# The x of the SSD head groups turned to tokens by VectorE block transposes and DRAM instead of TensorE, and the C·B products moved into a later visit

## The chip, the cores and the metric

The kernel runs on one core of a Trainium2 chip. The time is that of the device in microseconds, for one execution of the whole program. The core has TensorE (PE, matmul), VectorE (DVE), ScalarE (ACT), GpSimd (POOL) and SyncE (SP); each has its own queue of instructions, which it takes in order, and semaphores join them. ACT, POOL and SP also issue DMA transfers.

## The reference, cut to what matters

One inference step of one decoder layer. 256 prompt tokens and 8 samples of 8 new tokens (320 tokens in all) with a width of 2048 go through one input projection, then through two kinds of head groups (a gated chunk MLP and a state space mixer), an output projection and a convolutional FFN.

```python
def decoder_layer(x, ...):
    h = rms_norm(x, norm_mix_pre)
    proj = h @ w_in                              # [a_u | a_v | z | x,B,C | dt]
    gate_out = chunk_spatial_gate(a_u, a_v, ...)
    ssm_out = ssd_mixer(z, xbc, dt_raw, ...)
    x = x + rms_norm(concat([gate_out, ssm_out]) @ w_out, norm_mix_post)
    return x + rms_norm(conv_ffn(rms_norm(x, ...), ...), ...)

def ssd_mixer(...):
    xbc = silu(causal_depthwise_conv(xbc))       # x: 2048 = 32 heads x 64, B and C: 4 groups x 128
    dt, a = softplus(dt_raw + dt_bias), -exp(a_log)
    ...                                          # y = ssd_scan(...) + d * x, times silu(z), RMS norm per group

def ssd_scan(x, dt, a, bm, cm, init_state):      # per chunk of 128 tokens
    xdt = x * dt                                 # token by token, head by head
    cb = einsum(C_t, B_s)                        # per group, tokens x tokens
    y_diag = (cb * decay) @ xdt
    states = einsum(B, decay_states, xdt)        # summed over the tokens of a chunk
    y_off  = C @ states_in * exp(da_cs)
```

The 32 heads form four groups of eight heads; a group shares its B and C. All sums here run over tokens, so x is wanted with tokens on the partitions, while the projection leaves it with features on the partitions and tokens along the row.

## The kernel before

**The stream of weights.** All matrix products with weights are done in three float32r products: each operand is split into a rounded part and a rest, and whi·xhi, whi·xlo and wlo·xhi are added up in PSUM (`accumulate`, lines 134 to 136). Weights come in slabs of 512 KB (`slab`): SP loads one (`wraw`), ACT rounds it (`whi`, line 123), VectorE subtracts (`wlo`, line 124). There are three buffers of each, and a slab feeds 24 matmuls of 128 x 320. `project` computes columns of the input projection or of the FFN's up projection into four PSUM banks, with an eviction function for each (`scaled`, whose evictions `ev` are line 393). `chunk_out` takes four blocks of 128 rows of the output or the down projection; its 16 column blocks (`pd`) are added by VectorE to an accumulator in SBUF (line 247).

**Side work.** Everything else is written as generators that stand in two lists. Behind each slab, `tick` lets the tasks of `side` and the first one of `bg` go one step further. A task yields a pair: how many matmuls of weights have to be made before its next step, and how many have to be left in the running projection. `finish` drives a task to its end. `tc.issue_after` keeps an instruction behind a given one.

**Order of the stages around the change.** First come the v columns, dt, B and C, then the gate stage: x of group 0 is projected (`heads_in(0)`, which leaves it in a tile `xs`, features on partitions), and four gate groups follow, each with a projection of u (`gate_up`), the mixing inside chunks (`gate_mix`, which loads `wT` by POOL at line 786 and multiplies it by a mask at line 791) and a `chunk_out`. Then the four SSD groups: while the generator `ssd(g)` runs as a background task, the stream computes x of group g+1 (`heads_in_next`), `chunk_out` of an earlier group and z of group g (`heads_out`).

**B.** B is turned to tokens before the gate stage by `to_tokens`: for each of five blocks of 64 tokens VectorE transposes 32 x 32 squares (line 421) into a tile of the tag `pv` (four buffers, which evictions use too), and POOL writes it in four DMAs of 32 KB to DRAM (`b_d`, line 423), from where POOL loads rows of tokens (`b_raw`, line 831). B of the samples, four times repeated (`b4`, lines 839 to 843), is loaded in the gate stage.

**One SSD group, `ssd(g)`.** It works in visits between slabs.

- Visit one: for each of the two prompt chunks TensorE transposes four blocks of `xs` into PSUM (`by_token`, line 415), VectorE multiplies by dt out of PSUM (`times`, line 911, into `xdt`), and POOL makes a decayed copy of the first (`x0d`, line 916). Then the four products of C and B (lines 946 and 949), and their masks on VectorE. Before it, ACT writes the samples' x four times side by side (`fourfold`, line 432).
- Visit two, 48 matmuls later or more: eight transposes of that fourfold copy into two PSUM banks, the state's product of the first chunk (`s1`, line 968, from `x0d`), and 32 small products of C with the samples' states (line 977). Its PSUM is multiplied by dt for the samples (`samples_split`, `samples_rows`).
- Then 13 short steps n = 0 to 12 (12 for group 3): decays, the samples' new states (`grown`), and at n = 6 and n = 12 the products of y (line 1058). After them POOL makes `x1d`, the decayed copy of the second chunk (`decayed(1, 1)`), and SP stores it with `s1` for groups 0 to 2 (`x1_d`, `s1_d`); `load_ends` brings them back before the last chunk of the output projection.

Group 0 has a further visit in between, for `b_of_samples` (lines 860 to 867).

## Time and profile before

| | us |
|---|---|
| three runs | 1757.96, 1758.81, 1760.32 |
| median | 1758.81 |
| the profiled execution | 1759.16 |
| its span in the trace | 1757.5 |
| VectorE busy | 1171.2 |
| ScalarE busy | 826.8 |
| GpSimd busy | 325.5 |

The span goes from the first to the last instruction of the profiled execution; 1.66 us of its time lie around it. "Busy" is the sum of an engine's instructions; PE stands for TensorE's matmuls, PEld for its weight loads, which overlap them. The list of waits gives for each engine and line what ended its idle time. A group of instructions is given as line, engine, operation, output and inputs, the count, the busy time and the mean duration of one in nanoseconds, then the idle time ahead of it. In the timeline a row begins with the start and the time taken in microseconds; a count over one joins instructions in sequence, and a bracket gives the idle time before them and what ended it.

### The profile page before, as it was taken

Reading aid. Unit: us, or ns where it says so; the run is one execution under the profiler, and the core shown is the slowest. Engines: PE = TensorE matmul, PEld = TensorE weight load, DVE = VectorE, ACT = ScalarE, POOL = GpSimd, SP = SyncE. Lnnn points to the kernel's source line nnn. Section 1 sums busy time; section 2 is a strip of 40 time slices with the busy share of each in tenths; the row PEclk is TensorE's granted clock in tenths of the full one; section 3 lists DMA queues with packets and bytes.
Section 4 is the critical chain, followed back from the end, with each engine's and each line's share of the span. In section 5 each row is a group of like instructions: output and inputs, shape, how many; then the busy total and the mean of one; then the engine's idle time right before and its main releaser. Section 6 shows DMA issues by size and latency. Waiting matters only on the chain.

```text
span 1757.5 us, 31257 instructions
## 1 busy us (share of the span) xinstructions
PE 1748.8 (100%) x12129; PEld 1727.8 (98%) x12129; DVE 1171.2 (67%) x2004; ACT 826.8 (47%) x1218; POOL 325.5 (19%) x687
## 2 busy tenths in 40 slices
PE   9999999999999999999999999999999999999998
PEld 9999999999999999999999999999999999999998
DVE  6548863656969787778855566565657565656575
ACT  5444545334656565645544434343434343333445
POOL 2432330000413323111210101010201010101004
PEclk9999999999999999999999999999999999999999
DMA  7786554456676676665654545545554545454542
GB/s 236 228 239 186 181 175 148 153 164 191 194 217 204 213 220 188 213 196 161 187 157 146 157 147 156 148 151 153 154 149 149 155 149 155 149 155 147 155 150 106
DMA packets 229108, 302.26 MB, mean 172 GB/s; under 512 B 21344, under 2 KB 154336, under 8 KB 228768
## 3 DMA queue, kind: packets, MB, share of 16 engines
q1 hardware_dynamic: 213488, 274.09, 51.4%
q0 software_dynamic: 5888, 12.79, 2.5%
q10 hardware_dynamic: 9584, 13.38, 2.1%
q8 instruction: 96, 1.57, 0.4%
q14 instruction: 52, 0.43, 0.1%
HBM read 280.51 MB, written 19.69 MB: 171 GB/s over the span
## 4 chain that ended last, share of the span: by engine, by line
PE 60%; DVE 0%; issue 0%; ACT 0%; ACTq 0%
PE ps L134 13%; PE ps L136 12%; PE ps L135 12%; PE pd L135 7%; PE pd L136 7%; PE pd L134 7%; PE x1p L1402 0%; PE fin_ps L1130 0%; PE y_ps L1058 0%; PE tsum L292 0%; PE ps_other L136 0%; PE ps_other L134 0%; PE ps_other L135 0%; PE ps L188 0%; PE yo_ps L977 0%; PE up_ps L994 0%
## 5 line engine op out<-in xcount | busy, mean ns | idle before, releaser
L124 DVE TENSOR_TENSOR wlo<-wraw,whi 128x1024 fp32r<-128x1024 f32 (+2 forms) x480 | 582.9, 1215 | 418.2 <-ACT whi L123 414.0
L123 ACT CAST whi<-wraw 128x1024 fp32r<-128x1024 f32 (+2 forms) x479 | 495.6, 1035 | 663.9 <-PE ps L135 382.6
L134 PE MATMUL ps<-h_hi,whi 128*128 128x320 f32 x2428 | 750.8, 310 | 0.6 <-DVE acc_mix L247 0.6
L135 PE MATMUL ps<-h_lo,whi 128*128 128x320 f32 x2428 | 749.2, 309 | 0.0
L136 PE MATMUL ps<-h_hi,wlo 128*128 128x320 f32 x2428 | 748.5, 309 | 0.0
L134 PEld LDWEIGHTS ps<-h_hi,whi 128*128 128x128 f32 x2428 | 455.8, 188 | 3.5 <-issue 0.8
L135 PEld LDWEIGHTS ps<-h_lo,whi 128*128 128x128 f32 x2428 | 456.0, 188 | 0.4
L136 PEld LDWEIGHTS ps<-h_hi,wlo 128*128 128x128 f32 x2428 | 455.8, 188 | 0.0
L135 PE MATMUL pd<-flo,whi 128*128 128x320 f32 x704 | 217.2, 308 | 0.0
L136 PE MATMUL pd<-fhi,wlo 128*128 128x320 f32 x704 | 217.2, 308 | 0.0
L134 PE MATMUL pd<-fhi,whi 128*128 128x320 f32 x704 | 217.1, 308 | 0.0
L134 PE MATMUL pd<-ohi,whi 128*128 128x320 f32 x448 | 138.9, 310 | 0.1
L135 PE MATMUL pd<-olo,whi 128*128 128x320 f32 x448 | 138.4, 309 | 0.0
L136 PE MATMUL pd<-ohi,wlo 128*128 128x320 f32 x448 | 138.4, 309 | 0.0
L135 PEld LDWEIGHTS pd<-flo,whi 128*128 128x128 f32 x704 | 132.2, 188 | 0.0
L136 PEld LDWEIGHTS pd<-fhi,wlo 128*128 128x128 f32 x704 | 132.2, 188 | 0.0
L134 PEld LDWEIGHTS pd<-fhi,whi 128*128 128x128 f32 x704 | 132.2, 188 | 0.0
L1304 POOL COPY ptf<-pad 128x2 f32<-128x2 f32 x88 | 21.0, 238 | 599.6 <-DVE pad L1292 598.9
L247 DVE TENSOR_TENSOR acc_ffn<-acc_ffn,pd 128x320 f32<-128x320 f32 (+1 forms) x161 | 77.6, 482 | 37.2 <-PE pd L136 35.7
L134 PEld LDWEIGHTS pd<-ohi,whi 128*128 128x128 f32 x448 | 84.1, 188 | 0.9 <-PE pd L136 0.3
L135 PEld LDWEIGHTS pd<-olo,whi 128*128 128x128 f32 x448 | 84.1, 188 | 0.3
L136 PEld LDWEIGHTS pd<-ohi,wlo 128*128 128x128 f32 x448 | 84.1, 188 | 0.0
(339 smaller groups left out, 1756.1 us busy)
## 6 DMA issues: line engine op xcount, KB each, us to landing
wraw<-in_ffn_w_up SPq DMA_DIRECT2D x176, 512.0 KB, 3.6
wraw<-in_w_in SPq DMA_DIRECT2D x132, 512.0 KB, 3.9
wraw<-in_ffn_w_down SPq DMA_DIRECT2D x88, 512.0 KB, 3.3
wraw<-in_w_out SPq DMA_DIRECT2D x64, 512.0 KB, 3.4
st<-in_state_ssm SPq DMA_DIRECT2D x40, 256.0 KB, 4.3
out_ssm_state_sample<-st ACTq DMA_DIRECT2D x30, 256.0 KB, 2.5
cs<-dacs_d SPq DMA_DIRECT2D x16, 320.0 KB, 4.8
wraw<-in_w_in SPq DMA_DIRECT2D x12, 384.0 KB, 3.6
```

What stands on the lines that cost most here:

```text
L123: rounded[:] = [act.copy(hi, raw).ins]
L124: dve.tensor_tensor(out=lo, in0=raw, in1=hi.bitcast(F32), op=ALU.subtract)
L134: pe.matmul(ps, whi, xhi, start=first, stop=False)
L135: pe.matmul(ps, whi, xlo, start=False, stop=False)
L136: last_made[0] = pe.matmul(ps, wlo, xhi, start=False, stop=last).ins
L247: added_last[:] = [dve.tensor_tensor(out=acc[:, nb, ts], in0=acc[:, nb, ts], in1=ps[:, ts], op=ALU.add).ins]
L1304: pool.tensor_copy(ptf[:, k, :], pad[:, 256:258])
```

## The change

x of every group goes the way that B went: block transposes on VectorE, 20 POOL writes of 32 KB to DRAM (`x_d`, one tile for each group), and POOL loads of rows of tokens. `to_tokens` gets the writing function as an argument and runs as a task of `side`. The 64 transposes of TensorE and the eight fourfold copies of ACT are gone; `times` reads SBUF, in two halves, with the features in the order in which the block transposes leave them. Group 0's rows are loaded in the gate stage, where B of the samples was; that load moves into `ssd(0)` and `b_of_samples` behind visit two. For the other groups the rows are asked for at step n = 11 of the group before. The products of C and B move from visit one into visit two, their masks behind it; the multiplications of the samples move ahead of it. `x1d` is made and stored at n = 3.

```diff
+    x_d = [dr.tile([NT, 512], F32, name=f"x_d{g}") for g in range(4)]
...
-    def by_token(ps, x, c):
-
-        pe.transpose(ps, x[:, P * c:P * c + P], ident)
+    def by_pool(rows, o, t):
+
+        for i in range(4):
+            pool.dma_start(rows[o:o + NS, P * i:P * i + P].rearrange("(r t) f -> t r f", t=32), t[32 * i:32 * i + 32])
-    def to_tokens(x, rows):
+    def to_tokens(x, rows, by):
...
+            by(rows, o, t)
             yield
...
             finish(b_turned)
+            x_turned = {0: to_tokens(x0, x_d[0], by_pool)}
+            side.append(x_turned[0])
...
                     if g == 2:
-                        b4 = [[tp.tile([P, NT], F32, tag="pv", name="b4", bufs=4)[:, :256] for _ in range(2)] for _ in range(2)]
+                        finish(x_turned[0])
+                        x_raw = [[tp.tile([P, NT], F32, tag="pv", name="x_raw", bufs=4)[:, :256] for _ in range(2)] for _ in range(2)]
+                        for c in range(2):
                             for h in range(2):
-                                pool.dma_start(b4[i][h], b_d[o:o + 32, 256 * h:256 * h + 256].unsqueeze(0).broadcast_to([4, 32, 256]))
+                                pool.dma_start(x_raw[c][h], x_d[0][P * c:P * c + P, 256 * h:256 * h + 256])
...
+            def load_x_tokens(g):
+
+                raw = [sd.tile([P, 512], F32, tag="xde", name="x_raw", bufs=2) for _ in range(2)]
+                for c in range(2):
+                    pool.dma_start(raw[c], x_d[g][P * c:P * c + P])
+                return [[raw[c][:, 256 * h:256 * h + 256] for h in range(2)] for c in range(2)]
+
+            def load_x_samples(g):
+
+                x4 = sd.tile([P, 2, 512], F32, tag="xsp", name="x4", bufs=1)
+                for i in range(2):
+                    o = NP + 32 * i
+                    pool.dma_start(x4[:, i], x_d[g][o:o + 32].unsqueeze(0).broadcast_to([4, 32, 512]))
+                return x4
+
+            tokens_of = {0: x_raw}
+            samples_of = {0: load_x_samples(0)}
...
-                def times(out, ps, c, at=slice(0, P), h=slice(0, 8)):
+                def times(out, raw, c, h, at=slice(0, P), js=slice(0, 4)):
+
+                    n = js.stop - js.start
+                    o = out.rearrange("p (j h i f) -> p h j i f", j=4, h=2, f=32)[:, h, js]
+                    d = dt[at, c, h0:h0 + 8].rearrange("p (j h) -> p h j", h=2)[:, h, js]
+                    dve.tensor_tensor(out=o, in0=raw.rearrange("p (i j f) -> p j i f", j=4, f=32)[:, js],
+                                      in1=d.unsqueeze(2).unsqueeze(3).to_broadcast([at.stop - at.start, n, 2, 32]), op=ALU.mult)
...
+                raw = tokens_of.pop(g)
                 for c in range(2):
-                    ps = misc("xt_ps")
-                    for j in range(4):
-                        by_token(ps[:, P * j:P * j + P], xs[:, j], c)
-                    times(xdt[:, c, :], ps, c)
+                    for h in range(2):
+                        times(xdt[:, c, :], raw[c][h], c, h)
                     if c == 0:
                         x0d = decayed(0, 0)
-                ps = misc("cb_ps")
-                ...
...
+                yield 24, 0
                 if g == 0:
+                    b4 = load_b()
                     yield 48, 0
-                    with tc.issue_after(last_made[0]):
-                        b_of_samples()
-                yield 48, 72
-
-                ps_x = [x_of_samples(i) for i in range(2)]
+                with tc.issue_after(last_made[0]):
+                    xq = [samples_times(0)]
+                    for i in range(2):
+                        samples_rows(i)
+                yield 24, 72
+
+                ps_cb = misc("cb_ps")
+                ...
                 ps_s = misc("s1_ps")
                 pe.matmul(ps_s, btok[:, 0, bs], x0d, start=True, stop=True)
...
-                samples_split(0, ps_x[0])
+                masked()
                 act.copy(s1, ps_s)
                 yield 24, 0
+                if g == 0:
+                    with tc.issue_after(last_made[0]):
+                        b_of_samples(b4)
+                    yield 24, 0
...
                     if n == 0:
-                        samples_split(1, ps_x[1])
+                        xq.append(samples_times(1))
+                        samples_split(0, xq[0])
                     if n == 1:
-                        for i in range(2):
-                            samples_rows(i, ps_x[i])
+                        samples_split(1, xq[1])
                         yo_to_xdt()
+                    if n == 3:
+                        x1d = decayed(1, 1)
+                        if g < 3:
+                            with tc.issue_after(last_made[0]):
+                                sp.dma_start(x1_d[g], x1d)
+                    if n == 11 and g < 3:
+                        finish(x_turned[g + 1])
+                        with tc.issue_after(last_made[0]):
+                            tokens_of[g + 1] = load_x_tokens(g + 1)
+                            samples_of[g + 1] = load_x_samples(g + 1)
...
-                x1d = decayed(1, 1)
...
-                    sp.dma_start(x1_d[g], x1d)
...
                 x_of[g] = heads_in(g)
+                x_turned[g] = to_tokens(x_of[g], x_d[g], by_pool)
+                side.append(x_turned[g])
                 bg.append(tasks[g])
```

More of the change, by code (lines that the diff above doesn't have):

```diff
@@ L421, in to_tokens @@
             dve.transpose(out=t.rearrange("p r (j f) -> p r j f", j=4), in_=x[:, :, o:o + NS].rearrange("p j (r t) -> p r j t", t=32))
-            for i in range(4):
-                pool.dma_start(rows[o:o + NS, P * i:P * i + P].rearrange("(r t) f -> t r f", t=32), t[32 * i:32 * i + 32])
+            by(rows, o, t)
             yield
@@ L428, in in_order @@
         return ap.rearrange("p (i j f) -> p j i f", j=4, f=32)
-    def fourfold(out, x, i):
-        act.copy(out.rearrange("p k (q t) -> p k q t", q=4), x[:, :, NP + 32 * i:NP + 32 * i + 32].unsqueeze(2).to_broadcast([P, 4, 4, 32]))
-        return out
     with ExitStack() as mctx:
@@ L859, in hybrid_step, with load_b, b_of_samples @@
                 act.copy(btok[:, c].rearrange("p (j i f) -> p j i f", j=4, f=32), in_order(b_raw[:, 512 * c:512 * c + 512]))
-            def b_of_samples():
+            def load_b():
+                b4 = [[tp.tile([P, NT], F32, tag="pv", name="b4", bufs=4)[:, :256] for _ in range(2)] for _ in range(2)]
+                for i in range(2):
+                    o = NP + 32 * i
+                    for h in range(2):
+                        pool.dma_start(b4[i][h], b_d[o:o + 32, 256 * h:256 * h + 256].unsqueeze(0).broadcast_to([4, 32, 256]))
+                return b4
+            def b_of_samples(b4):
                 for i in range(2):
@@ L948, in ssd @@
-                for r in range(2):
-                    pe.matmul(ps[64 * r:64 * r + 64, NP:NT], bT[:, g, NP:NT], cT[:, g, NP:NT], start=True, stop=True,
-                              tile_position=(0, 64 * r))
-                dve.tensor_tensor(out=cb[:, NS:NT].rearrange("p (c t) -> p c t", c=2),
-                                  in0=ps[:, :NP].rearrange("p (c t) -> p c t", c=2),
-                                  in1=upper.unsqueeze(1).to_broadcast([P, 2, P]), op=ALU.mult)
-                dve.tensor_tensor(out=cb[NS:, :NS], in0=ps[NS:, NP:NT], in1=upper_s[NS:], op=ALU.mult)
```

47 lines of the change are left out of this document (25 added, 22 removed).

## The prediction

> **What bounds the kernel now.** I read the page's busy lines first, then the waits of PE, which name all of its idle time.
>
> ```profile
> span 1757.5 us, 31257 instructions
> PE 1748.8 (100%) x12129; PEld 1727.8 (98%) x12129; DVE 1171.2 (67%) x2004; ACT 826.8 (47%) x1218; POOL 325.5 (19%) x687
> ...
> PE early L69 <- DVE ones L65: 1.1, 1, 1.1
> PE ps_v L136 <- DVE wlo L124: 0.8, 2, 0.4
> PE ps L134 <- DVE acc_mix L247: 0.6, 1, 0.6
> ```
>
> The last three rows give microseconds, count and the mean of one. TensorE is busy for the whole span; these three waits are 2.5 us together, and only 0.8 us of them is for a weight split. So the end moves in two ways: by TensorE work that goes away, one for one, and by new waits of TensorE. What the other engines do costs nothing until it makes TensorE wait. The profiled run's own time is 1759.16 (span 1757.5 and 1.66 around it), 0.35 above the median of 1758.81.
>
> **What TensorE loses.**
>
> ```profile
> L415 PE MATMUL xt_ps<-ident,xs 128*128 128x128 f32 x32 | 4.1, 272 | 0.0
> L415 PE MATMUL xt_ps<-ident,x 128*128 128x128 f32 x32 | 4.1, 272 | 0.0
> ...
> 423.68 0.31 PE L136 MATMUL ps<-h_hi,wlo 128*128 128x320 f32 x1
> 423.83 1.03 PE L415 MATMUL xt_ps<-ident,xs 128*128 128x128 f32 x8
> 424.70 0.61 PE L946 MATMUL cb_ps<-cT,bT 128*128 128x128 f32 x4
> 425.24 0.34 PE L949 MATMUL cb_ps<-cT,bT 128*64 128x64 f32 x4
> 425.51 0.41 PE L134 MATMUL ps<-h_hi,whi 128*128 128x320 f32 x1
> 425.76 0.31 PE L135 MATMUL ps<-h_lo,whi 128*128 128x320 f32 x1
> ...
> 439.69 1.03 PE L415 MATMUL xt_ps<-ident,x 128*128 128x128 f32 x8
> 440.56 1.02 PE L968 MATMUL s_ps<-xde,btok 128*128 128x512 f32 x2
> ```
>
> Matmuls overlap, so I count from start to start. Eight transposes take 0.87 (423.83 to 424.70, and again 439.69 to 440.56). Each group has two such eights: 1.74. The first weight matmul behind a visit takes 0.25 (425.51 to 425.76) where a weight matmul otherwise takes 0.15 (423.68 to 423.83); with C·B in visit two there is one return less, 0.10. The C·B products themselves are moved and cost the same. In the changed kernel's order of instructions they stand directly ahead of the s1 product in groups 0 to 2, but eight weight matmuls ahead of it in group 3, so the return is saved three times. Sum: 8 x 0.87 + 3 x 0.10 = **7.3 us less**. The busy time of the two groups, 4.1 + 4.1 = 8.2, is the upper end, 7.0 (transposes alone) the lower.
>
> **What VectorE, ScalarE and GpSimd get.**
>
> ```profile
> L911 DVE TENSOR_TENSOR xdt<-xt_ps,dt x24: 411/426/693, 426.9 to 692.0; 32x256 f32<-32x256 f32 x16, 128x512 f32<-128x512 f32 x8
> L421 DVE STREAM_TRANSPOSE turned<-bT x5: 402/432/446, 241.2 to 247.6; 128x256 f32<-128x256 f32 x5
> L867 DVE TENSOR_TENSOR bsp<-b,bsp x8: 415/420/423, 429.1 to 433.4; 32x256 fp32r<-32x256 f32 x8
> 591.00:676.00 85.00, 85.00 (x635) 82.25 (x634) 69.40 (x125) 50.66 (x93) 22.48 (x25) 1.00 0.70 214
> 426.64 1.14 ACT L432 COPY x<-xs 128x512 f32<-128x512 f32 x2
> ```
>
> Before, a group has two multiplications xdt and two xq of 0.69 and four rows of 0.43 out of PSUM: 4.5 us. After, it has eight halves (128 x 256, from SBUF), eight smaller pieces of rows and five block transposes of 0.43. A half isn't in the trace: nearest are 0.42 (256 columns from SBUF on 32 partitions, L867; an instruction's length goes by columns, as the 32-partition and 128-partition forms of L911 show) and, above, 0.69 for a whole one. I take 0.42 for a half and, from the same row by columns, about 0.25 for a piece of 128. That is 8 x 0.42 + 8 x 0.25 + 5 x 0.43 = 7.5, **3 us more per group**. The fourth row is a stretch of 85 us that holds all of group 2 (its columns: length, busy time of PE, PEld, DVE, ACT and POOL, granted clock 1.00, DMA share, GB/s). DVE is idle for 15.6 of 85 there; 3 us fit, and I cost them at nothing. What hides them is the weight split's lead over TensorE; were DVE's lead gone, each microsecond of them would be one of TensorE. ACT loses 1.14 a group. POOL gets 24 or more DMA issues of about 0.54, 13 us, on 22.5 of 85: room enough on average. Behind them in POOL's order stand the multiplications for the products (cpx) and the states; they are consumed several slabs of 3.5 us later. I cost that at nothing as well. DMA carries 0.7 of its time in this stretch; the 20 writes and the loads are some 1.3 MB in 85 us, 15 GB/s beside 214.
>
> The store of x1 moves nine steps forward on SP's queue, between weight loads. It waits there for a POOL multiplication, and the loads behind it wait too; three buffers of weights, 10 us, cover it.
>
> **What has to be there in time.** The new wait is VectorE's, for the loaded rows; behind it on VectorE stand evictions and weight splits, and TensorE waits for those. Group 0's rows are asked for in the gate stage. Groups 1 and 2 have their writes while the group before still runs:
>
> ```profile
> 573.85 1.11 POOL L1038 TENSOR_TENSOR cpx<-cpx,cT 128x256 f32<-128x256 f32 x1 [5.63 <-ACT cpx L1037]
> ...
> L911 DVE TENSOR_TENSOR xdt<-xt_ps,dt x2: 681/687/693, 591.5 to 592.2; 128x512 f32<-128x512 f32 x2
> ```
>
> The second row is group 2's first use of x, at 591.5. The changed order puts the writes of x ahead of the multiplication of 573.85; even behind it they would be done, by the 11.7 and 4.7 worked out next, at 573.85 + 1.11 + 11.7 + 4.7 = 591.4. I cost groups 0 to 2 at nothing. If this fails in group 2, each microsecond goes on to TensorE. Group 3 has little:
>
> ```profile
> 669.41 0.48 DVE L247 TENSOR_TENSOR acc_mix<-acc_mix,pd 128x320 f32<-128x320 f32 x1
> ...
> 241.97 4.80 POOL L423 DMA_DIRECT2D b_d<-turned  x9 [2.19 <-DVE turned L421]
> 247.88 5.79 POOL L423 DMA_DIRECT2D b_d<-turned  x11 [1.11 <-issue]
> 253.65 0.59 POOL L831 DMA_DIRECT2D b_raw<-b_d  x1
> 254.82 0.55 POOL L831 DMA_DIRECT2D b_raw<-b_d  x1 [0.58 <-DMA b_d<-turned]
> ...
> b_d<-turned POOLq DMA_DIRECT2D x20, 32.0 KB, 2.5
> ...
> DMA to landing us min/median/max: 4.2/4.7/5.2
> ...
> L916 POOL TENSOR_TENSOR xde<-xdt,dec x8: 1044/1047/1091, 427.8 to 695.5; 128x512 f32<-128x512 f32 x8
> ...
> 685.87 1.04 PE L415 MATMUL xt_ps<-ident,x 128*128 128x128 f32 x8
> 686.74 1.02 PE L968 MATMUL s_ps<-xde,btok 128*128 128x512 f32 x2
> ```
>
> In the changed order VectorE's first transposes of group 3 stand behind the accumulation of 669.41. It ends at 669.9, and a transpose of 0.43 makes it 670.3. Twenty writes take as long as the twenty of b: 241.97 to 253.65, 11.7, of which 1.1 was idle. The load of the first rows is issued at 682.0 and lands 4.7 later (256 KB, the landing row is b_raw's): 686.7. Two halves of 0.42 make 687.5, the decayed copy on POOL (x0d, L916) 1.05: **688.6**.
>
> TensorE wants it at 686.74 before. Minus visit one (0.87 of transposes, 0.81 of C·B, 0.10 of return) and the eight transposes of 685.87, plus C·B 0.91 which now lies ahead, plus eight weight matmuls at 0.15 which the order puts there: 686.2. The wait is 2.4; I take **2.5**. Its ends: 0.9 with no idle among the writes and a landing of 4.2; 5 with a landing of 5.2 and idle in POOL's queue double. TensorE is in order, so the weight matmuls behind the product wait with it, and nothing later gives the time back.
>
> A rule speaks against this part. The Trainium skill ("SBUF — State Buffer", "Who interferes with whom") says that a VectorE instruction with two SBUF inputs and a GpSimd instruction that reads SBUF exclude each other; `times` now has two SBUF inputs where it had PSUM. The trace's nearest rows:
>
> ```profile
> 523.88 7.84 POOL L988 TENSOR_TENSOR st<-st,tote 128x512 f32<-128x512 f32 x6 [11.35 <-PE yo_ps L977]
> 524.75 1.44 DVE L930 TENSOR_TENSOR xsp<-xq,xsp 64x512 fp32r<-64x512 f32 x1
> 526.66 0.65 DVE L911 TENSOR_TENSOR xq<-xt_ps,dt 128x512 f32<-128x512 f32 x1
> ```
>
> With POOL busy, the subtraction with both inputs in SBUF takes 1.44, the multiplication out of PSUM 0.65. The trace agrees with the rule. By it x0d could stand behind a half, 0.4 later, 1754.8 in place of 1754.4; without it the sum stays as it is.
>
> **The sum:** 1759.16 - 7.3 + 2.5 = 1754.4 for a run like the profiled one, 1754.0 against the median.
>
> **The rivals.**
>
> *No wait in group 3.* The load lands earlier than b_raw's did, or the writes need less. For it: the landing's 4.7 comes from a load issued right behind its writes, part of which may be waiting for them. Against: the fastest landing, 4.2, still leaves 0.9. Time: 1759.16 - 7.3 - 0.35 = 1751.5; if also the 0.6 wait for acc_mix goes, 1750.9. By a fit that the Trainium skill gives for loads from GpSimd ("DMA: Bandwidth & Descriptors", "Anatomy of one DMA — SWDGE (gpsimd) path"), 256 KB would be there after an estimated 2.6, and the wait 0.4: 1751.9. The landing row of 4.2 to 5.2 contradicts it here.
>
> *The gate stage waits.*
>
> ```profile
> 257.62 0.54 POOL L786 DMA_DIRECT2D wT<-in_gate_wT  x1 [2.25 <-PE sg L803]
> 268.15 0.49 DVE L393 TENSOR_TENSOR ev<-ps,r 128x320 f32<-128x320 f32 x1 [0.92 <-PE ps L136]
> ...
> 261.72 0.69 DVE L791 TENSOR_TENSOR wT<-wT,upper 128x512 f32<-128x512 f32 x1 [1.34 <-DMA wT<-in_gate_wT]
> 270.32 1.22 DVE L124 TENSOR_TENSOR wlo<-wraw,whi 128x1024 fp32r<-128x1024 f32 x1
> 273.23 0.31 PE L134 MATMUL pd<-ohi,whi 128*128 128x320 f32 x1
> ```
>
> The changed order puts the 20 writes of x ahead of wT's load on POOL: from 255.4 (the last row of b_raw) to 267.1 instead of 257.62. It took 4.1 from there to the multiplication (257.62 to 261.72), so VectorE waits until 271.2, then multiplies (0.69), and an eviction (0.49) that stands behind it frees the bank that TensorE takes at 273.23. That is 272.4, a margin of 0.8; the split of 1.22 behind it comes to 273.6. Writes that take 3 us longer turn the margin into a wait of 2.2: 1754.0 + 2.2 = 1756.2.
>
> *Slower: the writes go by landings.* If POOL's queue admits only eight software transfers at a time (b's gap of 1.11 falls behind the ninth issue), twenty writes take 20 x L/8, with L the landing of one. At b's 2.5 this doesn't bind; at L = 8, where weight loads (DMA 0.70) crowd the same engines, they take 20. Then group 3's load lands 8.3 later and the wait is about 11: 1758.8 - 7.3 + 11 = 1762.5. It decides from a wait of 7.3, L = 6.2. Against: b's writes went beside the same weight loads.
>
> *It doesn't do what it says:* rows asked a step ahead are too late in every group, not only in group 3. Against it stands the bound of 591.4 for group 2. A delay of 3 us in each of two groups gives 1760; it is inside the rest below.
>
> **How the numbers follow.** Main case 0.42, with 1752.5 (wait 0.9) to 1756.5 (wait 5) as its own bounds; no wait 0.22; gate stage 0.14; slow writes 0.10; the rest, unforeseen waits of a few us, about 1757 to 1760, 0.12. The range from 1750.8 to 1758.6 leaves out the slow writes and part of the rest. A measurement tells 0.2%, 3.5 us, from no change: faster means below 1755.3, slower above 1762.3. Faster: 0.34 of the main case, 0.22, and 0.06 of the gate stage, 0.62. Slower: 0.06 of slow writes, 0.05 of the rest, 0.11. The same: 0.27.
>
> **What would show it.** Right: no transposes for x on PE and its busy time 7 us lower; one new PE wait, of 2 to 3 us, for the s1 product on POOL in group 3; about 12 us for each twenty writes; wT's multiplication near 271. Wrong: a PE wait on wlo in the stages of the groups (then VectorE's 3 us aren't hidden), on an eviction near 273, or on x4 or xdt in groups 0 to 2; or no wait at 686.

## The result and the profile after

The changed kernel takes 1783.14 us (median of 4 runs, 1781.48 to 1787.00), the kernel before 1759.14 beside it on the same chip: a ratio of 1.0135 with a 95% interval from 1.0122 to 1.0147. It is 24 us slower, where 5 us faster was forecast. The profiled execution is the slowest of the four, 1787.0 us with a span of 1785.3, so its losses add up to 27.8 us of span.

The page of the changed kernel, its span, busy line and DMA line, then from its list of waits those of TensorE (microseconds in all, times, longest):

```profile
span 1785.3 us, 31340 instructions
PE 1754.6 (98%) x12065; PEld 1725.9 (97%) x12065; DVE 1191.9 (67%) x2056; ACT 823.9 (46%) x1212; POOL 377.4 (21%) x785
...
DMA packets 234517, 309.09 MB, mean 173 GB/s; under 512 B 24448, under 2 KB 157440, under 8 KB 234176
...
PE s_ps L990 <- POOL xde L940: 6.8, 1, 6.8
PE ps L136 <- DVE wlo L124: 5.3, 6, 1.3
PE yo_ps L1006 <- DMA st<-in_state_ssm: 3.8, 3, 1.4
PE ps L134 <- ACT whi L123: 3.3, 2, 2.4
PE up_ps L1023 <- DVE xsp L954: 2.8, 1, 2.8
```

The 64 matmuls are gone (12129 to 12065). TensorE idles 30.7 us (1785.3 - 1754.6) where it idled 8.7: 22.0 more, which is the sum of these five rows; the kernel before has none of them. (Its own list of waits names 3.3 us of the 8.7, and not all of its idle time, as the prediction has it.) Its busy time should be 7.3 lower and is 5.8 higher, so the matmuls that remain took 13.1 us longer. What most of that is, three stretches behind one of the waits show (length, busy time and count of PE, PEld, DVE, ACT, POOL, then granted clock, DMA share, GB/s), with the timeline of TensorE beside them:

```profile
444.00:448.00 4.00, 1.75 (x8) 0.38 (x8) 3.94 (x4) 1.26 (x3) 3.85 (x4) 0.58 0.58 203
448.00:450.00 2.00, 1.87 (x9) 1.06 (x10) 2.00 (x3) 1.97 (x3) 1.57 (x1) 0.50 0.10 23
450.00:452.00 2.00, 2.00 (x11) 2.00 (x10) 1.96 (x7) 1.20 (x4) 0.85 (x1) 0.62 0.82 269
```

```profile
448.13 1.08 PE L1006 MATMUL yo_ps<-st,cb_cms 128*32 128x256 f32 x6 [1.03 <-DMA st<-in_state_ssm]
...
450.64 0.47 PE L136 MATMUL ps<-h_hi,wlo 128*128 128x320 f32 x1
450.90 0.47 PE L134 MATMUL ps<-h_hi,whi 128*128 128x320 f32 x1
...
451.62 0.31 PE L134 MATMUL ps<-h_hi,whi 128*128 128x320 f32 x1
451.76 0.31 PE L135 MATMUL ps<-h_lo,whi 128*128 128x320 f32 x1
```

A weight matmul starts 0.26 behind the last one while the clock is at 0.50, and 0.14 to 0.15 behind it from 451.6 on. So a wait of TensorE costs more than its own length. The granted clock was 0.50 in four stretches (444.7 to 451.5, 629.0 to 635.8, 707.5 to 714.3 and 728.0 to 731.4), 23.8 us in all, of which TensorE was busy for 17.8. At half speed that is at most 8.9 us of the 13.1; where the other 4 arose is not shown.

The Trainium skill ("TensorE: Matmul & The Clock Gate", "🔬 Part 1: The HAM clock gate (the "warmup" mystery)") says that the clock is halved after an idle window of some 3.4 us and comes back after some 3.4 us of sustained work. The trace agrees on the return, with about 3.5 us from 448.1 to 451.6. An unbroken idle window was not needed here: none of the three waits was longer than 1.4 us, and in the 3.4 us ahead of 444.7 TensorE was busy for 1.30.

**Where the 27.8 us arose.** The matmuls of 320 columns, all weight matmuls among them, are the same 11398 in the same order in both traces, so the start of the n-th in one less that in the other tells how late the stream is. It is level at the end of the gate stage, 6.8 us late behind group 0's visits, 11.8 behind group 1's, 18.3 behind group 2's, 29.3 behind group 3's, and 28.6 at the end.

*Group 0.* The timelines of VectorE and ScalarE, and the DMA issues from 426 to 438 us (KB each, median us from issue to landing), the changed kernel's and then those of before:

```profile
434.09 0.43 DVE L935 TENSOR_TENSOR xq<-x,dt 128x256 f32<-128x256 f32 x1 [5.75 <-DMA x<-x_d]
...
437.93 0.83 ACT L872 CAST bsp<-b 128x256 fp32r<-128x256 f32 x2 [9.48 <-DMA b<-b_d]
```

```profile
st<-in_state_ssm SPq DMA_DIRECT2D x5, 256.0 KB, 8.9
wraw<-in_w_in SPq DMA_DIRECT2D x2, 512.0 KB, 8.8
b<-b_d POOLq DMA_DIRECT2D x4, 128.0 KB, 10.5
x<-x_d POOLq DMA_DIRECT2D x1, 256.0 KB, 10.2
```

```profile
st<-in_state_ssm SPq DMA_DIRECT2D x6, 256.0 KB, 5.3
wraw<-in_w_in SPq DMA_DIRECT2D x2, 512.0 KB, 4.9
```

The samples' rows (`x4`, here x<-x_d) and those of B (`b4`) take over 10 us to land, and the weights and states that SP loads beside them 9 instead of 5. VectorE stands for x4 ahead of a weight split, ScalarE for b4 ahead of a rounding. Of TensorE's own waits in these visits three are for the late states (3.8 us) and one for a split (0.9).

*Group 1.* VectorE has lost its lead: TensorE waits three times for a split, 3.0 us. VectorE's pieces run beside POOL's multiplication of the states:

```profile
529.72 2.12 DVE L935 TENSOR_TENSOR xdt<-x,dt 32x128 f32<-32x128 f32 x2
...
529.32 7.98 POOL L1017 TENSOR_TENSOR st<-st,tote 128x512 f32<-128x512 f32 x6
```

```profile
L935 DVE TENSOR_TENSOR xdt<-x,dt x32: 272/281/1144, 436.0 to 721.9; 32x128 f32<-32x128 f32 x32
L935 DVE TENSOR_TENSOR xdt<-x_raw,dt x16: 409/418/1944, 426.9 to 709.4; 128x256 f32<-128x256 f32 x16
```

The last two rows are the forms of line 935 with their shortest, median and longest duration in ns. The medians, 0.28 and 0.42, are close to the estimates. The five pieces that ran beside a POOL multiplication took 1.05 to 1.14, the other 27 at most 0.29; a half beside POOL took up to 1.9. That is the rule of exclusion which the prediction cited from the Trainium skill ("SBUF — State Buffer", "Who interferes with whom"), with a larger price.

*Group 2.* The sums of the decays (`cs`) land late, 12.8 us after their issue (5.1 before, as the median of three), and ScalarE stands for them ahead of the next slab's rounding, for which TensorE waits 3.3 us (ScalarE's timeline, then two DMA issues from 590 to 620 us):

```profile
612.44 0.42 ACT L1070 ACTIVATE cpx<-cs 128x256 f32<-128x256 f32 x1 [14.08 <-DMA cs<-dacs_d]
```

```profile
x<-x_d POOLq DMA_DIRECT2D x2, 256.0 KB, 10.3
cs<-dacs_d SPq DMA_DIRECT2D x1, 320.0 KB, 12.8
```

*Group 3.* The timelines of POOL, VectorE and TensorE at the wait that was forecast:

```profile
689.91 4.30 POOL L417 DMA_DIRECT2D x_d<-turned  x8 [17.46 <-DVE turned L423]
...
698.28 4.21 POOL L417 DMA_DIRECT2D x_d<-turned  x8 [0.58 <-DVE acc_mix L247]
702.48 1.13 POOL L880 DMA_DIRECT2D x_raw<-x_d  x2
...
708.51 1.42 POOL L888 DMA_DIRECT2D x<-x_d  x2 [3.82 <-issue]
709.94 1.05 POOL L940 TENSOR_TENSOR xde<-xdt,dec 128x512 f32<-128x512 f32 x1
...
706.77 0.76 DVE L935 TENSOR_TENSOR xdt<-x_raw,dt 128x256 f32<-128x256 f32 x2 [3.77 <-DMA x_raw<-x_d]
...
711.04 2.07 PE L990 MATMUL s_ps<-xde,btok 128*128 128x512 f32 x2 [6.79 <-POOL xde L940]
```

Twenty writes take 12.6 us (11.7 reckoned), the rows land 4.3 after their issue (4.7), the two halves end at 707.5; then the issues of x4, which the prediction did not count, stand ahead of x0d on POOL until 709.94, 2.4 us. TensorE waits 6.8, not 2.5.

### The profile page after: what moved, and what is told of

It reads as the page before. It is cut to its first block, busy times and chain, and to the rows that moved or that the text cites. A ratio compares the mean times of both kernels' runs of the same rounds, so it can differ in the third digit from the quotient of the medians.

```text
span 1785.3 us, 31340 instructions
## 1 busy us (share of the span) xinstructions
PE 1754.6 (98%) x12065; PEld 1725.9 (97%) x12065; DVE 1191.9 (67%) x2056; ACT 823.9 (46%) x1212; POOL 377.4 (21%) x785
## 4 chain that ended last, share of the span: by engine, by line
PE 88%; DMA 5%; DVE 3%; issue 1%; POOL 1%; ACT 1%; SPq 0%; DVEq 0%; ACTq 0%; POOLq 0%
PE ps L134 18%; PE ps L136 18%; PE ps L135 18%; PE pd L134 10%; PE pd L135 10%; PE pd L136 10%; DMA cs<-dacs_d 2%; DVE wlo L124 1%; DMA wraw<-in_w_in 1%; DMA x_d<-turned 1%; PE y_ps L1091 1%; POOL x_d L417 1%; DMA b<-b_d 1%; ACT whi L123 0%; PE ps_v L136 0%
```

## The experiments

"Late" is the weight stream's lateness at its end in the profiled execution, as above. A profiled execution lies up to 4 us from its kernel's median, so it is good to 2 us or so. "Drain" is a last instruction of POOL, told of further down. "Before" is the median of the kernel before on the same chip.

| kernel | us | before | ratio (95%) | late | drain |
|---|---|---|---|---|---|
| changed | 1783.14 | 1759.14 | 1.0122 to 1.0147 | 28.6 | 2.2 |
| traffic | 1797.35 | 1759.64 | 1.0200 to 1.0231 | 38.0 | 2.1 |
| no_loads | 1782.30 | 1759.64 | 1.0114 to 1.0148 | 15.6 | 11.1 |
| no_writes | 1776.16 | 1759.64 | 1.0077 to 1.0108 | 12.4 | 7.2 |
| samples_late | 1786.76 | 1759.64 | 1.0132 to 1.0167 | 27.2 | 2.2 |
| b4_swap | 1781.74 | 1760.10 | 1.0105 to 1.0141 | 23.0 | 2.1 |
| swap_late | 1777.23 | 1760.10 | 1.0081 to 1.0113 | 19.5 | 2.1 |
| no_x4 | 1772.70 | 1759.51 | 1.0059 to 1.0088 | 4.0 | 11.3 |
| x4_behind | 1779.11 | 1759.51 | 1.0096 to 1.0124 | 18.5 | 2.1 |
| x4_plain | 1772.40 | 1759.02 | 1.0057 to 1.0087 | 17.4 | 4.0 |
| sp_writes | 1779.77 | 1759.02 | 1.0103 to 1.0130 | 19.3 | 5.4 |
| join_only | 1760.56 | 1760.10 | 0.9993 to 1.0012 | 0.5 | 4.1 |
| tokens_only | 1763.12 | 1760.10 | 1.0008 to 1.0027 | -0.2 | 8.5 |
| tokens_apart | 1762.50 | 1759.51 | 1.0010 to 1.0028 | -1.5 | 8.5 |
| tokens_all | 1764.39 | 1759.51 | 1.0021 to 1.0042 | 1.5 | 10.0 |
| tokens_sp | 1760.52 | 1759.02 | 0.9998 to 1.0016 | 1.4 | 4.6 |
| drain | 1763.89 | 1759.02 | 1.0015 to 1.0033 | 1.2 | 8.5 |
| drain_back | 1761.64 | 1759.87 | 1.0003 to 1.0021 | 3.2 | 2.2 |
| tokens_back | 1760.41 | 1759.87 | 0.9995 to 1.0013 | 3.0 | 2.2 |

**Traffic, loads, writes, or the samples' place?**

traffic is the kernel before with the transposes, writes and loads added; the loads go to a spare tensor in DRAM and nothing reads them.

```diff
+            def load_x(g):
+                for c in range(2):
+                    pool.dma_start(spare_d[g][P * c:P * c + P], x_d[g][P * c:P * c + P])
...
+                    if n == 11 and g < 3:
+                        finish(x_turned[g + 1])
+                        with tc.issue_after(last_made[0]):
+                            load_x(g + 1)
```

> The kernel before, with the changed kernel's transposes, its 80 writes of x and as many bytes loaded at the same places, but the loads go to a spare tensor in DRAM that nobody reads; TensorE's transposes stay. Theory A (the loads fill the DMA engines at the turn from one group to the next, and the state, sum and weight loads land late for the engines that take them in order): slower than before by 8 us or more, the sums' landing (cs, 4.8 us median before) with a longest of 8 us or more. Theory B (VectorE and ScalarE stand still for the new rows of x and b themselves, the traffic is harmless): within 3 us of before, 1757 to 1762.

It is 38 us slower, with the whole of TensorE's old work in place. But its cs loads land as before (3.5/4.9/6.1 as shortest, median, longest), so of theory A only the time came true. Its largest wait, 8.9 us for an operand that ScalarE writes (at 812 us, behind the groups), is none of the changed kernel's: copies from DRAM to DRAM are not the loads of the change. It shows that the added transfers alone can cost more than the change does, and not which.

no_loads and no_writes take the changed kernel and leave out, for groups 1 to 3, the loads of x (the multiplications read B's tile instead) or the writes (the loads read group 0's rows):

```diff
-                            tokens_of[g + 1] = load_x_tokens(g + 1)
-                            samples_of[g + 1] = load_x_samples(g + 1)
+                            tokens_of[g + 1] = [[btok[:, c, 256 * h:256 * h + 256] for h in range(2)] for c in range(2)]
+                            samples_of[g + 1] = btok
```

```diff
-                    pool.dma_start(raw[c], x_d[g][P * c:P * c + P])
+                    pool.dma_start(raw[c], x_d[0][P * c:P * c + P])
...
-                x_turned[g] = to_tokens(x_of[g], x_d[g], by_pool)
-                side.append(x_turned[g])
```

> The changed kernel without the loads of x for groups 1 to 3 (the multiplications read another tile in SBUF, so x of these groups is wrong); transposes and writes stay. Theories A and B: only group 0's loss is left, 1759.1 - 7.3 + 8.2 = 1760, at most 1764. Theory C (VectorE's three extra microseconds and the writes on POOL and DMA make the splits late): 1775 or more.

> The changed kernel without transposes and writes of x for groups 1 to 3 (their loads read group 0's tensor, so x of these groups is wrong); all loads stay at their places. Theories A and B: the loads still cost, 1772 to 1782, and group 3 gains some 4 us because its loads no longer wait for the writes. Theory C: 1764 or less.

Both take about half of the lateness away (28.6 to 15.6 and 12.4). no_writes, 1776.2, lies in the range of theories A and B. no_loads is hardly faster: its time of 1782.3 misses their range by 18 us and by itself speaks for theory C. But its stream is 13 us earlier than the changed kernel's, and what comes behind the last matmul takes 11.4 us in place of 4.1; "The end" tells why. In no_writes the x4 loads still land after 7.4 to 10.1 us, so the writes are not what makes them long. no_loads heals group 2: the stream loses nothing there. It doesn't heal group 1, which loses 7.8 us without its loads (6.8 with them, 3.5 in no_writes): there the loads are not the cause.

samples_late puts the samples' multiplications behind the masks again, where the kernel before has them:

```diff
-                with tc.issue_after(last_made[0]):
-                    xq = [samples_times(0)]
-                    for i in range(2):
-                        samples_rows(i)
...
-                        xq.append(samples_times(1))
+                        xq = [samples_times(0), samples_times(1)]
```

> The changed kernel with the samples' multiplications behind visit two, at n = 0 and 1, where they were before. Theory B: VectorE's wait for x4 no longer stands ahead of weight splits before visit two; 1770 or less. Theory A: the loads land as late as before and the waits move to others, 1777 to 1787.

Nothing is won by that alone; the time is in theory A's range. TensorE now waits 5.2 us for states in group 0, where it waited 3.8. In the changed kernel ScalarE's wait for b4 ends at 437.9, behind VectorE's for x4 at 434.1, so taking the second away leaves the first.

**Group 0: b4's place.** b4_swap loads b4 in the gate stage, as before, and group 0's x rows behind it; swap_late also takes samples_late's edit.

```diff
-                                pool.dma_start(x_raw[c][h], x_d[0][P * c:P * c + P, 256 * h:256 * h + 256])
+                                pool.dma_start(b4[i][h], b_d[o:o + 32, 256 * h:256 * h + 256].unsqueeze(0).broadcast_to([4, 32, 256]))
...
-            tokens_of = {0: x_raw}
+            tokens_of = {0: load_x_tokens(0)}
...
-                    b4 = load_b()
```

> The changed kernel with B of the samples loaded in the gate stage again, in the buffers where x of group 0's prompt was; that x is loaded when the groups begin, as many bytes at the same place. Theory D (in group 0, ScalarE stands for B's late rows ahead of a rounding, and VectorE for x4 ahead of a split; the weight stream stops): the ScalarE wait of 9.5 us is gone, group 0 loses 3 us or less in place of 8.5, and the time is 1775 to 1779. Theory A (the bytes at the turn count, whoever waits): 1781 to 1786 as the changed kernel.

> The one before, and the samples' multiplications behind visit two as well. Theory D: in group 0 nothing that stands ahead of a split waits for a broadcast load; its loss is below 1 us, the time 1772 to 1777. Theory A: as the changed kernel.

By the medians, each over its own before, the changed kernel is 24.0 us slower, samples_late 27.1, b4_swap 21.6 and both together 17.1; the lateness goes from 28.6 to 27.2, 23.0 and 19.5. So the two edits are worth 7 to 9 us, by the medians only together, which fits two waits of group 0 that lie over each other. b4_swap alone came out in theory A's range (1781.7), not in D's; swap_late is 0.2 above D's, and its group 0 still loses 3.2 us, with a wait of 2.4 for a state.

**The x4 loads.** From here on swap_late is the base. no_x4 leaves the samples' loads out (their multiplications read B's tile).

```diff
-            samples_of = {0: load_x_samples(0)}
+            samples_of = {0: btok}
...
-                            samples_of[g + 1] = load_x_samples(g + 1)
+                            samples_of[g + 1] = btok
```

> The kernel with B in the gate stage and the samples' multiplications late (1777.2), without the four-fold loads of the samples' x in any group (their multiplications read another tile in SBUF, so the samples' x is wrong). Theory A (the half megabyte of these loads, 9 to 11 us to landing, is what the DMA engines can't take at the turn): 1764 to 1769, group 0's gross loss 2 us or less in place of 5, group 3's wait for x0d 4 us. Rival (the multiplications from SBUF and the writes cost it): 1773 or more.

The lateness falls from 19.5 to 4.0, and groups 0 to 2 together lose 0.5 us where they lost 9.6. Group 3 still loses 5.5 (10.0), with a wait of 4.8 for x0d. The time misses theory A's range by 3.7 and is just short of the rival's: behind the last matmul it takes 11.6 us in place of 4.2, and without these 7.4 it would lie in A's range. What these eight loads do to the others, the DMA views of 426 to 438 us show, swap_late's first, then no_x4's:

```profile
GB/s 314 314 369 403 417 328 382 287 283 174 290 297 342 352 356 281 233 239 263 270 236 256 226 209 229 212 250 229 215 236 222 249 266 253 304 222 287 307 249 335
...
st<-in_state_ssm SPq DMA_DIRECT2D x6, 256.0 KB, 10.0
...
x<-x_d POOLq DMA_DIRECT2D x2, 256.0 KB, 11.2
...
cs<-dacs_d SPq DMA_DIRECT2D x1, 320.0 KB, 8.5
x_raw<-x_d POOLq DMA_DIRECT2D x1, 256.0 KB, 4.1
```

```profile
GB/s 410 382 300 328 287 246 314 379 331 307 335 399 399 365 396 406 362 345 225 225 215 287 304 321 382 382 386 341 270 195 137 75 61 181 335 369 273 352 410 294
...
st<-in_state_ssm SPq DMA_DIRECT2D x6, 256.0 KB, 6.0
...
cs<-dacs_d SPq DMA_DIRECT2D x1, 320.0 KB, 6.8
```

From 430.8 to 436.2, with x4 in flight, the DMA engines are busy throughout (a share of 1.08, since packets overlap) and move 239 GB/s; without it they move 261 at a share of 0.79, with slices over 380. The state loads take 10.0 instead of 6.0. An x4 load has the bytes of an x_raw load and takes 11.2, where x_raw took 4.1. But it also stands behind x_raw on POOL's queue, so these two numbers do not yet tell form from place. The form: x4 asks for 32 rows four times over. The Trainium skill ("DMA: Bandwidth & Descriptors", "🎯 Rules for kernel authors") says that a transfer whose outermost dimension is a broadcast of c copies runs on at most c of the 16 engines. The traces agree: where SP's queue has nothing in flight, two such loads have 4 to 8 packets in flight at a time (the changed kernel, 427.9 to 428.2 us), and plain loads of x_raw have 16 to 18 (swap_late, 427.4 to 427.9).

x4_plain tests the form: the same bytes in eight plain loads of 32 rows for each group.

```diff
-                    pool.dma_start(x4[:, i], x_d[g][o:o + 32].unsqueeze(0).broadcast_to([4, 32, 512]))
+                    for q in range(4):
+                        pool.dma_start(x4[32 * q:32 * q + 32, i], x_d[g][o:o + 32])
```

> The kernel with B in the gate stage and the samples' multiplications late (1777.2), with each four-fold load of the samples' x made of four plain loads of 32 rows (eight POOL issues a group in place of two, as many bytes). Theory G (the four-fold form is what is slow: its two loads move half as much per microsecond as the plain ones beside them): all of it lands within 6 us of the last issue and the time is 1765 to 1772. Rival (the bytes, or 32 partitions at a time): landings of 8 us or more, 1775 or more.

A plain load lands after 2.0/6.6/7.2 us (shortest, median, longest), but it has 64 KB; an x4 load of 256 KB takes 7.3/9.8/12.2 in swap_late. From the first issue of a group's x4 to its last landing it is 11.2, 10.4, 10.8 and 7.5 us in the four groups, instead of 12.9, 10.2, 12.7 and 11.9. The state loads take 8.0, between swap_late's 10.0 and no_x4's 6.0. The kernel is 13.4 us slower than its own before, where swap_late is 17.1, and the intervals of the two ratios overlap. Theory G is missed narrowly: 0.4 above its range, and up to 6.9 us from the last issue to the last landing instead of 6. Group 0 loses nothing now (swap_late 3.2), but group 1 loses 7.3 (3.5). The plain form does not give back all that no_x4 did: the bytes are still there, 32 issues take POOL's time, and group 3's waits, of which this is the list, remain:

```profile
PE up_ps L1020 <- DVE xsp L956: 5.6, 1, 5.6
PE ps L136 <- DVE wlo L124: 4.2, 4, 1.3
PE s_ps L987 <- POOL xde L942: 3.1, 1, 3.1
```

The form is worth 3.7 us by the medians and 2.1 by the stream, of the 15.5 by which no_x4 changes the stream; that is hardly more than these runs can tell from nothing. The rest goes with the loads' presence in either form.

**Group 3.** x4_behind asks for x4 of a group in visit one, behind x0d in the source, so that in group 3 it should no longer stand ahead of it:

```diff
-                            samples_of[g + 1] = load_x_samples(g + 1)
...
+                x4 = load_x_samples(g)
```

> The same kernel (1777.2) with the four-fold loads, asked for on POOL behind x0d, in the group itself, in place of ahead of it. If group 3's wait of 6.5 us for x0d is partly the two issues that stand ahead of it in POOL's order: the wait falls to 4 us and the time to 1772 to 1775. If the rows themselves are late: the wait stays at 6 and the time at 1776 or more.

The wait for x0d was 7.9, not 4, and the time 1779.1. But the run does not test what it was made for. POOL's timeline in group 3 still has both issues ahead of x0d, and so it is in the other groups:

```profile
697.68 0.72 POOL L889 DMA_DIRECT2D x<-x_d  x1 [2.30 <-DMA x_d<-turned]
701.02 0.70 POOL L889 DMA_DIRECT2D x<-x_d  x1 [2.62 <-issue]
701.74 1.05 POOL L940 TENSOR_TENSOR xde<-xdt,dec 128x512 f32<-128x512 f32 x1
```

sp_writes gives the writes of x to SP:

```diff
+    def by_sp(rows, o, t):
+        for i in range(4):
+            sp.dma_start(rows[o:o + NS, P * i:P * i + P].rearrange("(r t) f -> t r f", t=32), t[32 * i:32 * i + 32])
```

> The same kernel (1777.2) with the writes of x issued by SP in place of POOL. Theory H (group 3's wait for x0d comes from twenty issues and their landings on POOL's queue): the wait of 6.5 us falls to 3 us or less, and the time to 1769 to 1774. Rival (the rows are late because DMA is full): the wait stays at 5 or more, 1775 or more.

TensorE's waits in it:

```profile
PE up_ps L1024 <- DVE xsp L960: 7.1, 1, 7.1
...
PE s_ps L991 <- POOL xde L946: 1.1, 1, 1.1
```

The wait for x0d goes from swap_late's 6.5 to 1.1. Two things changed for it: the first rows are asked for at 690.5 instead of 694.4, and x4's issues now come behind x0d (707.9 behind 698.5), where swap_late has them ahead. no_x4, with the writes on POOL and no x4 at all, waits 4.8. So the writes on POOL's queue are the larger part of the wait, and x4's issues a smaller one. But x4 is late next (xsp, the samples' split), and the time is no better: 1779.8, 5.8 above the range.

**The parts of the change alone.** join_only is the kernel before with C·B moved into visit two. tokens_only brings the prompt's x of groups 0 to 2 by way of DRAM, with the samples and all of group 3 on TensorE as before, and C·B moved; tokens_apart is that with C·B in visit one; tokens_all is tokens_apart with group 3 by DRAM too.

```diff
-                ps = misc("cb_ps")
...
+                ps_cb = misc("cb_ps")
```

> The kernel before with only the products of C and B and their masks moved into visit two. All theories: between 0.5 us less and 1 us more than before; more than 3 us more would mean that the masks' new place is a cause of its own.

> The changed kernel with only the prompt tokens of groups 0 to 2 by DRAM (16 writes and two loads of 256 KB a group); the samples of every group and all of group 3 are transposed by TensorE and multiplied out of PSUM as before, with one visit for C and B. Saved on TensorE: 3 x 0.87 + 3 x 0.10 = 2.9. Theory E (the four-fold loads, their late landing and VectorE's multiplications from SBUF beside POOL cost the time): 1756 to 1761. Theory C (writes and transposes alone make the splits late): 1765 or more.

> The kernel with only the prompt tokens of groups 0 to 2 by DRAM (1763.1), with the products of C and B in visit one again, so that no fifth PSUM bank is asked for in visit two. Theory E: the waits of 1.4 us ahead of the states' products go, and the time is 1757 to 1759, 1 to 3 us below before. Rival (writes and transposes cost what the transposes on TensorE save): 1760 to 1763.

> The kernel before this one with group 3's prompt tokens by DRAM too, asked for at n = 11 of group 2. By the prediction's chain TensorE waits 2.5 us for x0d there and the time is 2 us above the one with groups 0 to 2. Theory F (the writes and their landings take longer than reckoned, and the wait brings a slower clock with it): a wait of 4 to 6 us and 5 to 8 us above it.

The join is worth nothing that can be measured (1.0003), as was expected. With it comes a wait of 1.4 us in visit two (two of them in tokens_only, 2.9 us), which tokens_apart does not have. That a fifth use of four shared PSUM banks makes it is read from the code; the trace names no releaser. tokens_only misses its range by 2.1 us. In tokens_apart the stream is 1.5 us ahead of the kernel before, 0.8 of it from before the groups, and no wait of TensorE has to do with x:

```profile
PE pd L134 <- DVE pad L461: 2.5, 4, 1.1
PE early L69 <- DVE ones L65: 1.1, 1, 1.1
PE ps_v L136 <- DVE wlo L124: 0.5, 1, 0.5
```

Yet it is 3 us slower than before, 3.5 above the upper end of what theory E expected and in the rival's range. tokens_all is 1.9 us above it (2 expected), and x0d of group 3 is waited for 1.1 us. It has 16 writes where no_x4 has twenty, and TensorE asks for the product some 2.5 us later; so with no x4 about the wait is 1.1 to 4.8.

**The end.** The last transfers of tokens_apart land at 1755.0 of a span of 1759.8. What ends it is a DRAIN of POOL that begins with its last work, at 1750.5, and lasts to 1759.0. Its length in each trace, by the number of DMAs that POOL issues:

```
DMAs of POOL   110   116   126   148   164   182   196    198    206         208   230
drain, us      4.10  4.59  5.40  7.20  8.51  9.98  11.12  11.28  2.05-2.14   2.22  4.01
```

0.0815 us for each DMA more ((11.28 - 4.10) / 88), and some 10 us less between 198 and 206. drain adds 54 small DMAs to the kernel before, drain_back 98 in all; tokens_sp is tokens_apart with its writes on SP (116 DMAs of POOL), tokens_back is tokens_apart with 44 small DMAs added.

```diff
+                        for i in range(54):
+                            pool.dma_start(spare_d[8 * i:8 * i + 8], b_d[8 * (i % 32):8 * (i % 32) + 8])
```

> The kernel before with 54 software transfers of 16 KB between tensors in DRAM, issued by GpSimd in the gate stage, which nobody reads: 164 in place of 110. Theory I: the weight stream is as before, GpSimd's drain at the end takes 8.5 us in place of 4.1 and the time is 1762.5 to 1764. Rival (the drain has another cause): within 1 us of before.

> The kernel with the prompt tokens of groups 0 to 2 by DRAM and C and B in visit one (1762.5, of which some 3.7 us are GpSimd's drain at the end behind 164 software transfers), with the 48 writes issued by SP: 116 software transfers. Theory I (the drain grows by 0.08 us with each software transfer): drain of 4.6 us in place of 8.5, time 1757.5 to 1759.5, at or 1 us below before. Rival: 1761 or more.

> The kernel before with 98 small DMAs of GpSimd added (208 in all, as many as the changed kernel has; 54 of them stood in the run drain, 44 more follow group 3's last state, where GpSimd idles for 36 us). Theory I, the drain at the end falls back once a count between 198 and 206 is passed: drain 2.0 to 2.5 us, time 1756.5 to 1760, so 4 to 7 us below the run drain although it has more DMAs. Theory J, the drain goes on growing by 0.0815 us a DMA, and the changed kernel's 2.2 came from something else: drain about 12, time 1766 to 1769.

> tokens_apart with 44 small DMAs added behind group 3's last state, 208 in all. Theory I: drain 2.0 to 2.5 in place of 8.51, so the stream's lead of 1.5 us at the FFN reaches the end: 1755 to 1758, the first version at or below the kernel before. Theory J: drain about 12, 1764 to 1767.

With 164 the drain was 8.505, with 208 it was 2.218, in the kernel before and in tokens_apart alike (2.220): the count sets it. The time of drain, 1763.9, is in theory I's range. The other times followed less than hoped. tokens_sp, with its drain of 4.6 as expected, is 1.0 above its range. It and tokens_back are level with the kernel before, and none of the versions beats it. drain_back is 1.8 us above before, though its drain is 1.9 shorter, and misses its range by 1.6, tokens_back misses by 2.4: both have a new wait of TensorE (1.4 and 1.3 us, for an operand that ScalarE writes) in the stage where the 44 issues stand on POOL, and with a short drain the last stores of y end the program (in the kernel before they land at 1756.4 of 1757.5, its drain ends at 1756.1).

## Why the prediction was wrong

- **TensorE's saving: right.** 64 matmuls are gone that took 7.0 us from start to start in the kernel before.
- **Durations: right where VectorE ran alone.** A half took 0.42, a piece 0.28 (0.25 reckoned), twenty writes 12.6 (11.7).
- **The gate stage: right.** wT was multiplied at 271.9 (271.2 forecast), and TensorE waited 0.2 us there.
- **"I cost groups 0 to 2 at nothing": the step that failed.** These groups made the stream 18.3 us late. The step rested on two numbers. The first was "15 GB/s beside 214", an average over 85 us, whose 1.3 MB come out only if x4 counts with the 128 KB that are read and not with the 512 KB that land. The rows come in bursts of 1 MB, and with x4 among them the DMA engines are busy for 90% or more in every slice from 429 to 438 us (swap_late), and the states and sums behind them come late. The second was one landing, b_raw's 4.7: x4 and b4, for which the prediction has none, take 7 to 13. By the runs x4 costs 15.5 us of stream, 4.5 of them in group 3; b4's late place and the samples' early place cost some 9.
- **The cover was VectorE's and ScalarE's lead, and the prediction priced its loss for VectorE alone.** Waits of 5.75 us of VectorE and 9.48 of ScalarE in one group use it up. That the 20.7 us of added VectorE work (12 reckoned) and the exclusion with POOL are then no longer free is argued from group 1, which loses 7.8 us in no_loads without its loads; no run takes them away alone.
- **Group 3's wait: right place, wrong size.** 6.8 in place of 2.5. By no_x4 (4.8) and sp_writes (1.1) the writes on POOL are the larger part of it; x4's issues ahead of x0d, 2.4 us, were left out of the sum. The upper bound of 5 comes to 4.1 by its own terms (2.5, 0.5 of landing, 1.1 of idle).
- **A wait of TensorE counted by its length.** 22.0 us of waits came with 13.1 us of longer matmuls, up to 8.9 of them by the clock.
- **The end was not priced.** Here it cost nothing: 208 DMAs of POOL drain in 2.2 us, and the last stores land behind that.
- The rival "slower: the writes go by landings" had the sign, by another mechanism: in group 3, where it was to decide, a write landed after 3.3 us (median) and the twenty took 12.6. (By its own terms it decides from L = 6.6, not 6.2.) "Rows a step ahead are too late in every group" came nearest, but it is the samples' rows, not the prompt's, and its price of 3 us a group was half of what group 0 alone lost.

The sum on the changed kernel's trace: -7.3 (matmuls) + 22.0 (waits) + 13.1 (longer matmuls, the remainder when the 7.3 is taken as given) = +27.8 of span. Open is where 4 of the 13.1 arose, how the 15.5 us of x4 divide exactly between its form and its bytes, what makes group 1's loss, and why tokens_back is not 2 us faster.

## What to carry to other kernels

Price a load by its moment and its form: look at the DMA share of the 12 us in which it will run, not at a stage's mean, take the landing from a row of the same access pattern, and ask which in-order engine stands for it ahead of the weight pipeline's next step, and whose loads it delays. When an engine that is busy for the whole span gets a wait, add the slow clock behind it. When an edit is meant to move an issue, look in the trace whether it moved. When a part of a change saves what it should and the time does not follow, look at what the program does after its last useful instruction.

## What the runs showed of the hardware that was not expected

- Two loads that each repeat 32 rows four times (256 KB each) had 4 to 8 packets in flight, plain loads 16 to 18. They land after 7.3/9.8/12.2 us (swap_late; shortest, median, longest) and slow loads of other queues (state loads 10.0 us, 6.0 without them). As plain loads of the same bytes they are there 7.5 to 11.2 us behind the first issue, instead of 10.2 to 12.9, and the state loads still take 8.0.
- VectorE's 32x128 multiplications with two SBUF inputs took 0.27 to 0.29 us alone and 1.05 to 1.14 beside a POOL multiplication.
- GpSimd's DRAIN at the end grows by 0.0815 us with each of its DMAs, from 4.10 at 110 to 11.28 at 198, is back at 2.05 to 2.14 at 206, and grows by as much again to 4.01 at 230.
- Waits of 1.0 to 1.4 us among small products were enough for the slow clock: TensorE was busy for 1.30 of the 3.40 us ahead of 444.7 and then ran at 0.50, back at full speed 3.5 us after the last wait's end.
